# Asking earlier for the operands of a Strassen-Winograd down projection, on one Trainium2 core

## The chip, the core and the metric

The kernel runs on one core of a Trainium2 chip. The metric is the device time of one execution in microseconds (us); a median of several runs stands for it. The engines are TensorE (PE, its weight loads PEld), VectorE (DVE), ScalarE (ACT), GpSimd (POOL) and SyncE (SP), which here issues the DMAs.

## The reference

One layer of a hybrid decoder on 512 tokens of 2048 channels, in float32:

```python
x = x + mix @ w_out[l]          # mix: two attentions and a convolution module
h2 = _rms_norm(x, norm2_g[l])
x = x + (jax.nn.silu(h2 @ w_gate[l]) * (h2 @ w_up[l])) @ w_down[l]
```

w_gate and w_up are 2048 x 5632, w_down is 5632 x 2048. The change concerns the last line alone.

## The kernel before

**The products.** Gate, up and down are each done as one level of Strassen-Winograd: a 2 x 2 block product with seven multiplications, numbered 1 to 7, whose operands are sums of blocks. Each multiplication keeps float32 accuracy by splitting both operands into a high and a low part (`wh`, `wl` for the weights) and spending three matmuls of 128x128 by 128x512: high by high, low by high, high by low. POOL makes the sums of weight blocks (L172), ACT the high parts (L269 `wn` in PSUM, L270 `wh`), DVE the low parts (L271 `wl`), always two units ahead of PE. A unit is one pair (`wh`, `wl`), with 12 matmuls, or 6 where it holds one 128-row pair of blocks in place of two.

**Gate and up** (`class Up`) run as 11 blocks n of 28 units: seven products twice (`blk.first` 0 and 4), two units each. What a block gives is weighted on POOL (L1258), turned on DVE (L1262) and stored to DRAM as `bd` (L1267). Later each half of it becomes a `Pair` p (0 to 21): eight reads of `bd` in 32-row pieces with turned axes (`p..l`, `p..r`, L1131), sums on POOL (L1144 to L1149), the split into seven pieces on ACT (L1112) and POOL (L1116), and the stores of these pieces to `od` (L1101). A piece a*q*_*p*, 128x512, is the operand of Down's product q for pair p.

**Down** (`class Down`) runs as 12 blocks t of seven products in the order 7, 1, 5, 6, 4, 2, 3, two units each. Blocks 2r and 2r + 1 use the pairs of range r: four pairs (0 to 3), three (4 to 6), four, three, four, four. The first of the two uses its pieces for one half of the output and the second lets go of them after the other half. The results are added into 16 sums `y`, which start as the turned residual in DRAM (`x2t`, loaded at L1312). Because seven weight tensors of a block live in a few buffers, a block's weights are loaded to buffers as the splits of other weights leave them (L243).

**What sets the order around the change.** `load_next(n, limit)` (L1302 ff.) takes the next n entries of the list `feed` and issues a DMA for each on SP: pieces (L1317) or sums `y` (L1312). The list begins with range 0's 28 pieces, with eight `y` after the products 7 and 1, then the other eight `y`, then the pieces of range 1, 2 and so on. In the last block of gate and up (n = 10) it is called after each unit from the fifth on; in Down after each unit with n = 1, as long as fewer than 46 pieces are held. `later(k, f, queue=extras)` puts a call k units ahead; the last block's two `Pair`s, 20 and 21, are started that way (L1240 to L1242).

SP issues all these DMAs in the order of the program: weight loads, pieces, `y`, reads of `bd`, stores to `od`. An entry whose buffer is not free holds up all behind it. The program gives SP's DMAs eight semaphores in turn, and each DMA waits until the one eight before it has landed. Pieces, `y` and the tiles of a `Pair` share 73 slots of 128x512.

Of the kernel before, what the change touches and what calls it, by code (L numbers as in the profile page):

```python
# [71 lines left out]
NBLOCKS = NP // 2  # L72
# [44 lines left out]
def kernel(ctx: ExitStack, tc: tile.TileContext, xT, wi, wo, wgu, wd, cst_in, outT):  # L117
# [20 lines left out]
    def slot(name, dt=F32, cols=T):  # L138
        return sp.tile([P, cols], dt, name=name, tag="s")
# [66 lines left out]
    for t, (g, r) in enumerate(DOWN):  # L206
        first, end = RANGES[r]
# [227 lines left out]
    for k in range(KT):  # L435
# [5 lines left out]
        if k == 0:  # L441

            at["use"] = 2
            first = [splits.pop(u) for u in range(2)]
# [15 lines left out]
        if k == 0:  # L460
# [5 lines left out]
            first = w = None  # L466
# [613 lines left out]
    def norm2():  # L1080

        b = psum["high"].tile([P, 1024], F32, name="r2s", tag="h")[:, :NT]
        n2["r"] = token_scale(ssum2, D, "n2", b)[1]
# [19 lines left out]
    def later(n, fn, *args, queue=evacs):  # L1103
        while len(queue) <= n:
            queue.append([])
        queue[n].append((fn, *args))
# [59 lines left out]
    class Up:  # L1166
# [43 lines left out]
        def done(self, first, q, banks):  # L1210
            if first and q == 7:
                self.c = {}
            by = self.keep if first else self.add
            for a, b in enumerate(banks):
                if q == 7:
                    by(1, 1, a, b)
                elif q == 1:
                    by(0, 0, a, b)
                elif q == 4:
                    by(1, 0, a, b)  # L1220
                elif q == 6:
                    by(0, 1, a, b)
                    self.less(0, a, b)
                    self.less(1, a, b)
                elif q == 5:
                    self.less(1, a, b)
                else:
                    self.add(0, q - 2, a, b)
            if first:
                return  # L1230
            if q in (6, 5):
                later(1, self.gate, 6 - q, queue=extras)
            elif q == 2:
                self.dram = tc.dram_tile([T, T], F32, name=f"bd{self.n}")
            if q in (2, 3):
                later(0, self.weigh, q - 2)
                later(2, self.turn, q - 2)
                later(3, self.store, q - 2, queue=extras)
            if q == 3:
                first, every = (25, 20) if self.n == NBLOCKS - 1 else (5, 13)  # L1240
                for at in range(2):
                    later(first + every * at, Pair, self.dram, 2 * self.n + at, at, queue=extras)  # L1242

# [43 lines left out]
    def turn_x2(key):  # L1287

        z = turns[key] = slot("z")
        for part in range(4):  # L1290
            nc.sync.dma_start(by_blocks(z, part), turned(x2d, key, part))
# [14 lines left out]
    def load_next(n, limit=99):  # L1306
        while feed and n and len(acts) < limit:
            key = feed.pop(0)
            n -= 1
            if len(key) == 4:  # L1310
                y[key] = slot("y")
                nc.sync.dma_start(y[key], x2t[key])  # L1312
            else:
                q, j = key
                acts[key] = slot(f"a{q}_{j}", F32R)
                at = LAID.index(q)
                nc.sync.dma_start(acts[key].bitcast(F32), od[j][:, at * T:(at + 1) * T])  # L1317

    for n in range(NBLOCKS):
        blk = Up(n)  # L1320
        for blk.first in (0, 4):
            for i, q in enumerate(ORDER):
                for c, _ in enumerate(blk.product(q)):
                    at_unit = (7 if blk.first else 0) * 2 + 2 * i + c
                    if ticks.due and at_unit % 2:
                        ticks.tick()
                    if n == 0 and at_unit == 12:
                        norm2()
                    if 1 <= n <= 8 and at_unit in (9, 23):
                        key = SUMS[2 * n - 2 + at_unit // 16]  # L1330
                        turn_x2(key)
                        later(6, turn_x2_now, key)
                    if n == NBLOCKS - 1 and at_unit > 3:
                        load_next(1)
                if n == NBLOCKS - 1:
                    for j in range(4):
                        ops.pop((q, blk.first + j))
# [240 lines left out]
```

## Time and profile before

| | |
|---|---|
| time, median of 3 runs | 1874.56 us (1872.96 to 1874.84) |
| profiled execution, its own time | 1872.51 us |
| its span | 1870.6 us |
| mean granted TensorE clock | 0.997 |
| PE busy | 1846.8 us, 99% of the span |
| DVE, ACT, POOL busy | 77%, 71%, 59% |
| HBM traffic over the span | 171 GB/s |
| Down, first to last matmul | 1422.3 to 1866.3 us of the span |

A row of the timeline reads: start, duration, engine, line, operation, names, and in brackets the idle time of the engine just before it and what ended it. A row of the windows view gives for a stretch of the span the busy time of each engine, the granted TensorE clock, the mean busy share of the DMA engines and the bytes that they moved per second. Rows of SPq are issues of DMAs; their duration is that of the issue and not of the transfer. In the chain of waits a DMA's piece runs from issue to landing.

### The profile page before, as it was taken

How to read it: one execution, taken by the hardware profiler on the slowest of the kernel's cores; microseconds unless marked ns; L12 is line 12 of the kernel's file. 1: busy time of each engine (PE TensorE's matmuls, PEld its weight loads, DVE VectorE, ACT ScalarE, POOL GpSimd, SP SyncE). 2: the span in 40 equal slices, each digit the busy share in tenths (PEclk: the TensorE clock that was granted, in tenths of full speed). 3: DMA queues.
4: the chain of work that ended last, by engine and by line, in shares of the span. 5: the costliest groups of instructions: out<-in, count | busy, mean ns of one | idle time of the engine just before them, and what ended most of it. 6: DMA issues, size and time to landing. Idle time of an engine off the chain costs nothing.

```text
span 1870.6 us, 26605 instructions
## 1 busy us (share of the span) xinstructions
PE 1846.8 (99%) x8370; PEld 1528.0 (82%) x8370; DVE 1432.9 (77%) x2052; ACT 1322.3 (71%) x1794; POOL 1106.7 (59%) x850
## 2 busy tenths in 40 slices
PE   9999999999999999999999999999999989899999
PEld 7888888888888888888888888888888768688887
DVE  6678878998689777777777777777777656677777
ACT  6345644553468778888888888888888667778775
POOL 0126533100003567776887777868778778878775
PEclk9999999999999999999999999999999999999999
DMA  7252253343343366786777776777588676766655
GB/s 272 69 153 82 84 144 98 94 127 123 130 141 109 107 168 175 200 223 175 208 207 193 210 203 189 213 184 220 164 266 262 220 238 197 247 218 232 221 185 113
DMA packets 382988, 330.36 MB, mean 177 GB/s; under 512 B 171648, under 2 KB 311552, under 8 KB 382848
## 3 DMA queue, kind: packets, MB, share of 16 engines
q1 hardware_dynamic: 382704, 328.66, 60.2%
q8 instruction: 66, 1.08, 0.2%
q14 instruction: 74, 0.61, 0.1%
q10 hardware_dynamic: 144, 0.01, 0.0%
HBM read 255.56 MB, written 64.63 MB: 171 GB/s over the span
## 4 chain that ended last, share of the span: by engine, by line
PE 93%; DMA 4%; POOL 1%; ACT 1%; issue 0%; SPq 0%; DVE 0%; POOLq 0%; ACTq 0%; DVEq 0%
PE out L1184 15%; PE out L1182 15%; PE out L1185 15%; PE out L1432 6%; PE out L1433 6%; PE out L1434 6%; PE o L310 3%; PE o L309 3%; PE o L308 3%; DMA a<-od 2%; PE cq L308 1%; PE cq L309 1%; PE cq L310 1%; PE ak L308 1%; PE aq L308 1%; PE av L308 1%
## 5 line engine op out<-in xcount | busy, mean ns | idle before, releaser
L1182 PE MATMUL out<-wh,h 128*128 128x512 f32 x1232 | 479.4, 389 | 0.0
L1185 PE MATMUL out<-wh,h 128*128 128x512 f32 x1232 | 479.3, 389 | 0.0
L1184 PE MATMUL out<-wl,h 128*128 128x512 f32 x1232 | 479.3, 389 | 0.0
L1182 PEld LDWEIGHTS out<-wh,h 128*128 128x128 f32 x1232 | 231.2, 188 | 48.1
L1184 PEld LDWEIGHTS out<-wl,h 128*128 128x128 f32 x1232 | 231.2, 188 | 48.0
L1185 PEld LDWEIGHTS out<-wh,h 128*128 128x128 f32 x1232 | 231.2, 188 | 47.9
L1432 PE MATMUL out<-wh,a 128*128 128x512 f32 x620 | 243.5, 393 | 15.7 <-DMA a<-od 12.1
L1433 PE MATMUL out<-wl,a 128*128 128x512 f32 x620 | 242.1, 390 | 0.5 <-DVE wl L271 0.5
L1434 PE MATMUL out<-wh,a 128*128 128x512 f32 x620 | 241.8, 390 | 0.0
L275 ACT CAST wh<-w 128x1024 fp32r<-128x1024 f32 (+2 forms) x94 | 97.0, 1033 | 152.2 <-PE o L309 64.7
L1432 PEld LDWEIGHTS out<-wh,a 128*128 128x128 f32 x620 | 117.2, 189 | 44.8 <-DMA a<-od 10.7
L253 DVE TENSOR_TENSOR wl<-w,wh 128x1024 fp32r<-128x1024 f32 (+2 forms) x95 | 113.4, 1193 | 40.6 <-ACT wh L275 37.8
L1433 PEld LDWEIGHTS out<-wl,a 128*128 128x128 f32 x620 | 117.4, 189 | 25.0 <-DVE wl L271 1.3
L1434 PEld LDWEIGHTS out<-wh,a 128*128 128x128 f32 x620 | 117.3, 189 | 24.4
L1442 DVE TENSOR_TENSOR y<-y,out 128x512 f32<-128x512 f32 x164 | 106.4, 684 | 35.8 <-PE out L1434 31.2
L519 DVE SCALAR_TENSOR_TENSOR y<-bu,cst,y 128x511 f32<-128x511 f32 (+14 forms) x120 | 90.0, 750 | 0.7
L308 PE MATMUL o<-mh_c,wh 128*128 128x512 f32 x128 | 51.1, 399 | 0.0
L308 PE MATMUL cq<-hh,wh 128*128 128x512 f32 x128 | 50.5, 395 | 0.0
L310 PE MATMUL o<-mh_c,wl 128*128 128x512 f32 x128 | 50.0, 391 | 0.0
L309 PE MATMUL cq<-hl,wh 128*128 128x512 f32 x128 | 49.9, 390 | 0.0
L309 PE MATMUL o<-ml_c,wh 128*128 128x512 f32 x128 | 49.9, 390 | 0.0
L310 PE MATMUL cq<-hh,wl 128*128 128x512 f32 x128 | 49.9, 390 | 0.0
(2376 smaller groups left out, 4883.1 us busy)
## 6 DMA issues: line engine op xcount, KB each, us to landing
od<-a SPq DMA_DIRECT2D x154, 256.0 KB, 4.2
a<-od SPq DMA_DIRECT2D x154, 256.0 KB, 5.8
w<-in_wi SPq DMA_DIRECT2D x58, 512.0 KB, 3.5
w<-in_wo SPq DMA_DIRECT2D x32, 512.0 KB, 3.4
x<-in_xT SPq DMA_DIRECT2D x16, 256.0 KB, 6.9
xr<-in_xT SPq DMA_DIRECT2D x16, 256.0 KB, 3.7
x2d<-xr SPq DMA_DIRECT2D x16, 256.0 KB, 2.0
z<-x2d SPq DMA_DIRECT2D x64, 64.0 KB, 4.0
```

The lines of the kernel that those rows point to most:

```text
L253: fn(*args)
L275: (nc.vector.tensor_copy if u == 0 else nc.scalar.copy)(hi[:, :n], t[:, :n])
L308: nc.tensor.matmul(out, wh, xh, start=start, stop=False)
L309: nc.tensor.matmul(out, wh, xl, start=False, stop=False)
L310: nc.tensor.matmul(out, wl, xh, start=False, stop=stop)
L1182: nc.tensor.matmul(b, x[:, high], wh[:, s], start=c == f == 0 and q in (7, 1, 5, 2), stop=False, skip_group_check=True)
L1184: nc.tensor.matmul(b, x[:, high], wl[:, s], start=False, stop=False, skip_group_check=True)
L1185: nc.tensor.matmul(b, x[:, low], wh[:, s], start=False, stop=c == f == 1, skip_group_check=True)
L1432: nc.tensor.matmul(b[:, lo:hi], x[:, high], wh[:, s], start=start, stop=False, skip_group_check=True)
L1433: nc.tensor.matmul(b[:, lo:hi], x[:, high], wl[:, s], start=False, stop=False, skip_group_check=True)
L1434: nc.tensor.matmul(b[:, lo:hi], x[:, low], wh[:, s], start=False, stop=last, skip_group_check=True)
L1442: getattr(eng, op)(t, t, src)
```

## The change

Two numbers change. In the last block of gate and up, `load_next` takes one and two entries in turn, so that 36 entries are asked for there in place of 24: all of range 0's pieces and eight `y`. And the last block's two `Pair`s start 34 and 54 units after the block, in place of 25 and 45.

```diff
             if q == 3:
-                first, every = (25, 20) if self.n == NBLOCKS - 1 else (5, 13)
+                first, every = (34, 20) if self.n == NBLOCKS - 1 else (5, 13)
                 for at in range(2):
                     later(first + every * at, Pair, self.dram, 2 * self.n + at, at, queue=extras)
...
                     if n == NBLOCKS - 1 and at_unit > 3:
-                        load_next(1)
+                        load_next(1 + at_unit % 2)
```

As Down's own rule of one entry a unit stays, every entry of the list that follows stands 12 units further ahead. No instruction is added or taken away. The order on PE and DVE is the same; it changes on SP, and on ACT and POOL by the two `Pair`s.

SP at the end of gate and up's last block, before. In a name such as a4_2 the first number is the product, the second the pair; w('22', 'd0B') is a weight block of Down's block 0, b10c the last block's result.

```order
L243 DMA w('22', 'd0B')_13886<-in_wd 128x4x256
L1317 DMA a6_2_13906<-od2_5904 128x512
L1317 DMA a6_3_13928<-od3_5905 128x512
L1317 DMA a4_0_13951<-od0_5902 128x512
L1317 DMA a4_1_13980<-od1_5903 128x512
L1267 DMA bd10_13885<-b10c100_13340 128x512
L1267 DMA bd10_13885<-b10c101_13342 128x512
L243 DMA w('12', 'd0A')_13999<-in_wd 128x4x256
L1317 DMA a4_2_14013<-od2_5904 128x512
```

The same place of the changed kernel:

```order
L243 DMA w('22', 'd0B')_13908<-in_wd 128x4x256
L1317 DMA a3_1_13928<-od1_5903 128x512
L1317 DMA a3_2_13950<-od2_5904 128x512
L1317 DMA a3_3_13952<-od3_5905 128x512
L1312 DMA y_13975<-x2t1100_5932 128x512
L1312 DMA y_14004<-x2t1101_5933 128x512
L1267 DMA bd10_13907<-b10c100_13342 128x512
L1267 DMA bd10_13907<-b10c101_13344 128x512
L243 DMA w('12', 'd0A')_14023<-in_wd 128x4x256
```

Down's block 0 ends with a3_3. Before, ten pieces from a4_2 to a3_3 stand behind the store of `bd` and the load of w('12', 'd0A'); now all stand ahead of both.

SP around the weights of Down's block 4 (pairs 7 to 10), before; p21l and p21r are the reads of `Pair` 21.

```order
L243 DMA w('21', 'd4A')_15049<-in_wd 128x4x256
L1317 DMA a1_7_15057<-od7_5909 128x512
L1101 DMA od20_5922<-a4_20_14991 128x512
L1317 DMA a1_8_15082<-od8_5910 128x512
L1131 DMA p21l_15084<-bd10_13885 32x16x32 x4
L1317 DMA a1_9_15102<-od9_5911 128x512
L243 DMA w('11', 'd4A')_15115<-in_wd 128x4x256
L243 DMA w('21', 'd4B')_15117<-in_wd 128x4x256
L1317 DMA a1_10_15131<-od10_5912 128x512
L1131 DMA p21r_15133<-bd10_13885 32x16x32 x4
L243 DMA w('11', 'd4B')_15145<-in_wd 128x4x256
```

And in the changed kernel:

```order
L243 DMA w('21', 'd4A')_15045<-in_wd 128x4x256
L1317 DMA a4_7_15053<-od7_5909 128x512
L1317 DMA a4_8_15081<-od8_5910 128x512
L1317 DMA a4_9_15098<-od9_5911 128x512
L243 DMA w('11', 'd4A')_15115<-in_wd 128x4x256
L243 DMA w('21', 'd4B')_15117<-in_wd 128x4x256
L1317 DMA a4_10_15131<-od10_5912 128x512
L1101 DMA od20_5922<-a2_20_15055 128x512
L1101 DMA od20_5922<-a3_20_15057 128x512
L243 DMA w('11', 'd4B')_15145<-in_wd 128x4x256
```

The pieces next to these weights are now those of the fifth product and no longer of the second, and the eight reads of `Pair` 21 are gone from between the weights.

POOL at the end of Down's block 3, before (the rows from the last sum for block 3 to the first sums for block 4; d3u is a result of product 1):

```order
L172 TENSOR_TENSOR w('11', 'd3B')_14810<-w('11', 'd3B')_14810,w('12', 'd3B')_15047 128x512
L1442 TENSOR_TENSOR y_13481<-y_13481,d3u0_15060 128x512
L1442 TENSOR_TENSOR y_13507<-y_13507,d3u1_15062 128x512
L172 TENSOR_TENSOR w('s', 'd4A')_15194<-w('21', 'd4A')_15049,w('11', 'd4A')_15115 128x1024
L172 TENSOR_TENSOR w('s', 'd4B')_15220<-w('21', 'd4B')_15117,w('11', 'd4B')_15145 128x1024
```

And in the changed kernel:

```order
L172 TENSOR_TENSOR w('11', 'd3B')_14824<-w('11', 'd3B')_14824,w('12', 'd3B')_15043 128x512
L1116 TENSOR_TENSOR a5_20_15155<-p20a_15032,a5_20_15155 128x4x2x32
L1116 TENSOR_TENSOR a6_20_15157<-p20a_15032,a6_20_15157 128x4x2x32
L1442 TENSOR_TENSOR y_13433<-y_13433,d3u0_15059 128x512
L1442 TENSOR_TENSOR y_13461<-y_13461,d3u1_15061 128x512
L172 TENSOR_TENSOR w('s', 'd4A')_15204<-w('21', 'd4A')_15045,w('11', 'd4A')_15115 128x1024
L172 TENSOR_TENSOR w('s', 'd4B')_15232<-w('21', 'd4B')_15117,w('11', 'd4B')_15145 128x1024
```

Between the sum of w('11', 'd3A') with w('21', 'd3A') and the first sum for block 4, w('s', 'd4A'), one POOL instruction of `Pair` 20 stood before (its last, a4_20); now the other ten stand there, and a4_20 follows w('s', 'd4B'). Those of `Pair` 21 move from the first to the second half of block 4 and the start of block 5.

## The prediction

> **What bounds the kernel now.** The first page gives the shares.
>
> ```profile
> PE 1846.8 (99%) x8370; PEld 1528.0 (82%) x8370; DVE 1432.9 (77%) x2052; ACT 1322.3 (71%) x1794; POOL 1106.7 (59%) x850
> ```
>
> TensorE is busy for 1846.8 of 1870.6 us, so work on another engine counts only where TensorE waits for it. What TensorE waits for in Down is summed in the waits view (total, times, longest), from which these are all the rows of the lines 1432 to 1434.
>
> ```profile
> PE out L1432 <- DMA a<-od: 12.1, 8, 2.4
> PE out L1432 <- ACT wh L270: 1.9, 2, 1.5
> PE out L1432 <- ACT wn L269: 1.6, 1, 1.6
> ...
> PE out L1433 <- DVE wl L271: 0.5, 1, 0.5
> ```
>
> In all 16.1 us and twelve waits, all between Down's first matmul and its block 5. Some of them in TensorE's rows of the timeline, and the first matmul of block 5:
>
> ```profile
> 1455.21 0.50 PE L1432 MATMUL out<-wh,a 128*128 128x512 f32 x1 [2.17 <-DMA a<-od]
> ...
> 1525.43 0.47 PE L1432 MATMUL out<-wh,a 128*128 128x512 f32 x1 [1.64 <-ACT wn L269]
> ...
> 1533.51 0.77 PE L1432 MATMUL out<-wh,a 128*128 128x512 f32 x1 [2.21 <-DMA a<-od]
> ...
> 1604.27 0.50 PE L1432 MATMUL out<-wh,a 128*128 128x512 f32 x1 [2.38 <-DMA a<-od]
> ...
> 1617.61 0.39 PE L1432 MATMUL out<-wh,a 128*128 128x512 f32 x1
> ```
>
> Eight waits are for pieces, with 12.1 us. I count the one at 1525.43 as a ninth although the view names ACT's L269: the piece that this matmul reads was issued as late as 1519.90 (below). So pieces cost 13.7 us; the three others are for a split (1.9 + 0.5 = 2.4 us). The nine lie at the ends of blocks 0, 2 and 4, the first blocks of a range. The windows view tells the rest of the loss, since matmuls behind a wait are also slower.
>
> ```profile
> 1422.00:1465.00 43.00, 39.06 (x171) 31.60 (x171) 29.23 (x34) 30.87 (x37) 41.56 (x29) 1.00 0.81 285
> 1465.00:1503.00 38.00, 38.00 (x168) 31.16 (x167) 26.13 (x30) 27.76 (x30) 27.00 (x16) 1.00 0.58 178
> 1503.00:1542.00 39.00, 32.32 (x129) 24.96 (x129) 22.87 (x30) 23.84 (x36) 31.58 (x26) 0.91 0.73 238
> 1570.50:1617.50 47.00, 41.46 (x169) 32.13 (x168) 28.13 (x32) 33.08 (x40) 45.01 (x32) 0.96 0.76 263
> 1537.00:1540.00 3.00, 3.00 (x7) 2.41 (x8) 0.00 (x0) 0.00 (x0) 1.43 (x2) 0.50 1.05 399
> ```
>
> The second row is block 1, without a wait: 38.00 / 168 = 0.226 us for a matmul. In the first, third and fourth TensorE is idle for 3.94 + 6.68 + 5.54 = 16.16 us, which is the twelve waits. Their matmuls take 39.06 + 32.32 + 41.46 = 112.84 us; 171 + 129 + 169 = 469 of them at 0.226 would take 106.1. So 6.7 us more go in slower matmuls: about half of it at the first matmul behind each wait (0.50 us in place of 0.39 as at 1617.61, and one start's overlap, 0.39 - 0.23, lost: 0.27 each, 3.2 for twelve), the other 3.5 us in two stretches in which the granted clock was 0.50: one around the last row (0.91 in the third window), one late in the fourth (0.96). **Waits and what follows them cost 16.2 + 6.7 = 22.9 us**, and no more is to be had in blocks 0 to 4.
>
> **Why pieces are late.** The queue of SP, at the end of gate and up's last block and in block 0:
>
> ```profile
> 1418.00 3.42 SPq L1317 DMA_DIRECT2D a<-od  x4
> 1425.00 0.91 SPq L1267 DMA_DIRECT2D bd<-b10c  x2
> 1434.33 0.38 SPq L243 DMA_DIRECT2D w('12', 'd0A')_13999<-in_wd  x1
> ...
> 1446.96 1.13 SPq L1317 DMA_DIRECT2D a<-od  x2
> ```
>
> After four pieces SP stands from 1421.4 until the last block's result can be stored (1425.00), then until 1434.33, when the buffer of w('12', 'd0A') comes free. Ten pieces of block 0 are behind. They then go out in a burst, and the chain of waits shows what a DMA costs in it:
>
> ```profile
> 1440.77 6.13 DMA od<-a
> ...
> 1446.96 8.20 DMA a<-od
> ```
>
> SP can't issue a DMA before the one eight ahead of it has landed: the store issued at 1440.77 lands at 1446.90, and the piece issued at 1446.96 takes 8.20 us and ends TensorE's wait at 1455.21. Eight issues in 1446.96 - 1440.77 = 6.19 us make 0.77 us for each. In blocks 2 and 4 the queue is short, but one entry a unit comes out of the list while a product of two units uses four (or three) pieces; the lead is spent at the block's end:
>
> ```profile
> 1510.70 0.40 SPq L243 DMA_DIRECT2D w('12', 'd2A')_14700<-in_wd  x1
> 1519.90 0.50 SPq L1317 DMA_DIRECT2D a<-od  x1
> ```
>
> The piece for the matmul at 1525.43 is asked for 5.5 us ahead, and a piece takes this long from issue to landing:
>
> ```profile
> a<-od SPq DMA_DIRECT2D x154, 256.0 KB, 5.8
> ```
>
> **The change, first term: all pieces earlier.** The order shows block 0's last piece, a3_3, ahead of the store at 1425.00, with its use in the last unit ahead of 1465, block 1's first matmul: over 30 us. a3_6, block 2's last, now stands ahead of w('12', 'd2A') (1510.70), some 20 us before its use; a3_10 stands ahead of w('12', 'd4A'):
>
> ```profile
> 1583.60 0.38 SPq L243 DMA_DIRECT2D w('12', 'd4A')_15343<-in_wd  x1
> ```
>
> over 20 us before block 4's last product. Against 5.8 us, or 8.2 in a burst, all nine waits go, with their starts (9 x 0.27 = 2.4) and the clock stretches that lie between them (3.5): 13.7 + 2.4 + 3.5 = **19.6 us**. Buffers don't hold this up: each moved piece takes the slot of one that TensorE let go of at least 15 us before its new place in the queue.
>
> **Second term: the `Pair`s.** The splits at 1573.71 to 1595.70 are late because POOL is:
>
> ```profile
> 1553.67 3.45 SPq L1131 DMA_DIRECT2D p21l<-bd  x4
> 1560.74 3.34 SPq L1131 DMA_DIRECT2D p21r<-bd  x4
> 1564.20 1.31 SPq L243 DMA_DIRECT2D w('11', 'd4B')_15145<-in_wd  x1
> ...
> 1558.77 2.56 POOL L1442 TENSOR_TENSOR y<-y,d3u 128x512 f32<-128x512 f32 x2 [1.60 <-DVE d3u L1458]
> 1563.24 2.40 POOL L172 TENSOR_TENSOR w('s', 'd4A')_15194<-w('21', 'd4A')_15049,w('11', 'd4A')_15115 128x1024 f32<-128x1024 f32 x1 [1.92 <-DMA w('11', 'd4A')_15115<-in_wd]
> 1569.24 2.39 POOL L172 TENSOR_TENSOR w('s', 'd4B')_15220<-w('21', 'd4B')_15117,w('11', 'd4B')_15145 128x1024 f32<-128x1024 f32 x1 [3.60 <-DMA w('11', 'd4B')_15145<-in_wd]
> ...
> 1574.08 0.74 POOL L1144 TENSOR_TENSOR p21a<-p21l 128x256 f32<-128x256 f32 x1
> ...
> 1586.04 1.44 POOL L1116 TENSOR_TENSOR a<-p21r,a 128x256 fp32r<-128x256 f32 x2
> ```
>
> Eight turned reads of `Pair` 21 hold SP for 3.45 + 3.34 us between block 4's weights, w('11', 'd4B') goes out at 1564.20, and POOL is idle 3.60 us for it. After that POOL is behind through block 4. The reads now come later, and `Pair` 21's sums go behind those that are needed. So the three split waits go: 2.4 + 3 x 0.27 = **3.2 us**. Against that, ten POOL instructions of `Pair` 20 now stand in block 3 ahead of w('s', 'd4A'), and one less behind: three sums and L1149 at 0.74, six splits (L1116) at 0.72, together 7.3, less the 0.74 that a4_20 took there. POOL's idle times of 1.60 and 1.92 us absorb half: 6.5 - 3.5 = 3.0 us, so w('s', 'd4A') is done at 1563.24 + 2.40 + 3.0 = 1568.6. ACT needs 2.0 us more for `wn` and `wh`, and block 4's first matmul stood at 1570.5 (where the fourth window begins): a wait of 0.1 to 0.3, with 0.27 for the start. Its bounds are 0 and 6.5 + 1565.6 + 2.0 - 1570.5 + 0.27 = 3.9 if POOL can use neither idle time. I take **0.6 us** lost. w('s', 'd4B') follows at 1571.0, where it was done at 1571.63 before: nothing further.
>
> **Third term: twelve more transfers in gate and up's last block.**
>
> ```profile
> 1384.00:1422.00 38.00, 38.00 (x169) 31.49 (x168) 28.55 (x32) 31.85 (x39) 29.44 (x21) 1.00 0.91 280
> ```
>
> This stretch has the busiest DMA engines before Down, 0.91. In it, by the timeline of POOL, ACT and TensorE:
>
> ```profile
> 1385.85 2.41 POOL L172 TENSOR_TENSOR w('21', 'u21A')_13257<-w('21', 'u21A')_13257,w('22', 'u21A')_13486 128x1024 f32<-128x1024 f32 x1 [6.50 <-DMA w('22', 'u21A')_13486<-in_wgu]
> 1396.61 1.05 ACT L270 CAST wh<-w('11', 'u21A')_13374 128x1024 fp32r<-128x1024 f32 x1
> 1400.51 0.39 PE L1182 MATMUL out<-wh,h 128*128 128x512 f32 x1
> ```
>
> POOL has waited 6.50 us for w('22', 'u21A'), and in the chain behind it the first high part is done at 1397.66 and used at 1400.51: 2.85 us to spare. By the order, three or four more pieces now stand ahead of that weight; at 0.77 us it lands 2.3 to 3.1 us later, and TensorE waits 0 to 0.3 with 0.27 for the start. The price of a transfer has bounds: 0.26 MB / 280 GB/s = 0.94 from this row, and 8.20 / 8 = 1.03 from the burst. At 1.03 four make 4.1 and the loss is 1.5 us; at the other end it is nothing. I take **0.4 us**. The remaining transfers are absorbed while SP stands from 1421.4 on. Block 0's first weights are two transfers later (1.5 us), and have room:
>
> ```profile
> 1431.88 2.42 POOL L172 TENSOR_TENSOR w('11', 'd0A')_13743<-w('21', 'd0A')_13636,w('11', 'd0A')_13743 128x1024 f32<-128x1024 f32 x1
> 1435.28 1.05 ACT L270 CAST wh<-w('11', 'd0A')_13743 128x1024 fp32r<-128x1024 f32 x1
> 1438.59 0.39 PE L1432 MATMUL out<-wh,a 128*128 128x512 f32 x1
> ```
>
> The high part is done at 1436.33, 2.26 us before its use: nothing.
>
> *The Trainium skill, "DMA: Bandwidth & Descriptors", section Specifications, gives an HBM limit of about 358 GB/s for a core. With nine pieces more in the 38 us, the 280 GB/s of the row become 280 + 9 x 0.262 MB / 38 us = 342, and by that limit nothing would be late at all; by the row's share of 0.91 the same bytes would need 1.11 of the DMA engines, some 4 us more than there are. The clock stretch above moved 399 GB/s at a share of 1.05, so the trace does not agree with the limit, and I go by the price of a transfer.*
>
> **The sum.** 19.6 + 3.2 - 0.6 - 0.4 = 21.8 us. From the profiled execution's own 1872.51 us: 1850.7. The median of the runs shown, 1874.56, is 2.05 above that execution: 1852.8, rounded 1853.
>
> **Rivals.**
>
> *POOL becomes the bound in blocks 3 and 4.* Block 3 lasts 28.6 us; POOL then has four sums of 128x1024 at 2.40, four half as large at about 1.2, eight additions at 1.28 and `Pair` 20's 7.3: 31.9 us. For it: 31.9 is over 28.6, by 3.3; a second shortage of the same size could come with `Pair` 21 at block 5's start. Against it: it has 5 us of lead at the block's start and the two idle times. It would give back 3.3 to 6.6 us: 1856.1 to 1859.4, in the middle 1857.8.
>
> *The half clock stays.* The trace ties 0.50 to stretches with two waits close together, and block 0, with a wait of 2.17 us, had 1.00. If it has another cause, 3.5 us stay: 1856.3. *The Trainium skill, "TensorE: Matmul & The Clock Gate", Part 1, has the clock fall after an idle window of about 3.4 us. No wait here is that long, 2.4 being the longest, yet the clock fell: by that rule the waits would not be the cause. The trace speaks more for waits, since no row outside their neighbourhood has 0.50.*
>
> *Only block 0 heals.* Down's own limit, 46 pieces held, could eat the twelve entries of lead by block 2. Then only 3.94 + 0.5 go, less 0.4: 1870.5. Against it: the order has the places after block 0 moved too.
>
> *The change doesn't do what it says.* If the DMA engines are what makes pieces late in blocks 2 and 4 (1.05 in the stretch at 0.50), asking earlier only moves the queue: 1874, no change.
>
> *Slower: weights of up's last block queue behind the twelve transfers.* One mechanism: each added piece ahead delays w('22', 'u21A') and all behind it by its price, and TensorE waits from 2.85 us on. To cancel 21.8 + 0.4 + 2.85, twelve transfers would have to cost 2.1 us each; 0.77 to 1.03 was measured. At 2.3 it gives 1876 to 1878.
>
> **How the numbers follow.** Forecast, 1853: 0.58. POOL: 0.18. Half clock: 0.06. Only block 0: 0.05. No change: 0.06. Slower: 0.04; something else, split among them: 0.03. The range reaches down to where all costs are nothing (1872.51 - 22.9 + 2.05 = 1851.7) and 2.7 below, for the runs' own 1.9 and shorter waits in later blocks that I haven't counted; upward to the POOL case with both shortages in full (1859.4), up's block at its upper end (1.1 more) and the spread of 2, about 1863; block 4's bound of 3.9 lies inside. It holds the first three cases. Faster by over 0.2% (3.7 us, about what a measurement of this kernel can tell from no change): 0.58 + 0.18 + 0.06 + 0.05 and a little of the rest, 0.88; within it 0.07; slower 0.05.
>
> **What would show it.** Right: TensorE's rows in blocks 0, 2 and 4 without a bracket from a<-od, block 0 to block 5's start shortened from 195 us (1422.3 to 1617.6) to about 172, no stretch at 0.50. The second term: POOL's w('s', 'd4B') without an idle time for DMA, and a bracket of under 0.5 us at block 4's first matmul. The third: a bracket at the product that uses w('11', 'u21A'), and nothing above 1.5 us. Wrong would be brackets from ACT or POOL of 4 us and more in blocks 3 to 5, or pieces still late there with the DMA share above 1.

## The result and the profile after

| | before | changed |
|---|---|---|
| median of the runs | 1873.76 us (4 runs) | 1853.13 us (4 runs, 1851.65 to 1853.89) |
| ratio, with its 95% interval | | 0.9889 (0.9872 to 0.9906) |
| profiled execution, its own time | 1872.51 us | 1851.65 us |
| TensorE's clock below full, inside Down | 1533.3 to 1540.1, 1605.0 to 1608.4 | 1546.1 to 1549.6 |
| first matmul of Down | 1422.27 | 1420.75 |

The changed kernel is 20.6 us faster, where 21.6 was forecast from the median shown then (1874.56). All that the waits view of the changed kernel lists for TensorE (total, times, longest):

```profile
PE idle L332 <- DVE ones L342: 1.1, 1, 1.1
PE out L1432 <- DVE y L1442: 0.9, 1, 0.9
PE out L1433 <- DVE wl L271: 0.7, 1, 0.7
PE sides L1397 <- DVE y L1411: 0.7, 1, 0.7
PE out L1432 <- ACT wh L270: 0.7, 1, 0.7
```

No row is left that waits for a<-od: 12.1 us in eight waits before. L332 and L1397 lie at the kernel's start and end. The three other waits follow each other in block 3; in the timeline of TensorE, with the first matmuls of blocks 3, 4 and 5:

```profile
1525.47 0.39 PE L1432 MATMUL out<-wh,a 128*128 128x512 f32 x1
...
1541.24 0.50 PE L1432 MATMUL out<-wh,a 128*128 128x512 f32 x1 [0.65 <-ACT wh L270]
...
1543.76 0.49 PE L1432 MATMUL out<-wh,a 128*128 128x512 f32 x1 [0.87 <-DVE y L1442]
...
1544.94 0.50 PE L1433 MATMUL out<-wl,a 128*128 128x512 f32 x1 [0.69 <-DVE wl L271]
...
1558.73 0.39 PE L1432 MATMUL out<-wh,a 128*128 128x512 f32 x1
...
1596.81 0.39 PE L1432 MATMUL out<-wh,a 128*128 128x512 f32 x1
```

The bracket at 1543.76 names DVE's addition, but w('22', 'd3A') came to ACT late as well: its high part was done at 1543.70 (the row of L270 is quoted below). The windows view, for the stretch before Down and for blocks 0, 3 and 4:

```profile
1384.00:1422.00 38.00, 38.00 (x169) 31.45 (x168) 28.04 (x33) 31.62 (x39) 29.41 (x22) 1.00 1.03 322
1420.70:1458.80 38.10, 38.10 (x169) 31.55 (x169) 27.70 (x34) 29.24 (x37) 35.58 (x28) 1.00 0.85 300
1525.40:1558.70 33.30, 31.09 (x128) 24.71 (x127) 21.90 (x29) 23.19 (x36) 30.64 (x25) 0.95 0.80 269
1558.70:1596.80 38.10, 38.10 (x169) 31.53 (x168) 28.20 (x32) 32.36 (x39) 37.94 (x28) 1.00 0.91 282
```

Blocks 0 and 4 have TensorE busy throughout. Block 3 has the idle 2.21 us of the three waits and a mean clock of 0.95. The first matmul of each block gives its length (before, it stood at 1422.27, 1464.91, 1503.28, 1541.92, 1570.48 and 1617.61):

| us | block 0 | 1 | 2 | 3 | 4 | sum |
|---|---|---|---|---|---|---|
| before | 42.64 | 38.37 | 38.64 | 28.56 | 47.13 | 195.34 |
| changed | 38.08 | 38.08 | 28.56 | 33.26 | 38.08 | 176.06 |
| difference | -4.56 | -0.29 | -10.08 | +4.70 | -9.05 | -19.28 |

So 24.0 us are gone from blocks 0, 1, 2 and 4, and 4.7 are given back in block 3. From block 5 on nothing differs. The two profiled executions are 20.86 us apart; the 1.5 us beyond the table lie ahead of Down, and not at the change: within the first 700 us TensorE was idle for 3.10 us in one and 1.12 in the other.

Where block 3's 4.70 us come from is seen on SP and POOL, in the changed kernel:

```profile
1515.16 3.44 SPq L1131 DMA_DIRECT2D p20l<-bd  x4
1520.86 1.97 SPq L1131 DMA_DIRECT2D p20r<-bd  x4
1522.94 1.06 SPq L243 DMA_DIRECT2D w('22', 'd3A')_14893<-in_wd  x1
...
1527.90 2.41 POOL L172 TENSOR_TENSOR w('21', 'd3A')_14739<-w('21', 'd3A')_14739,w('22', 'd3A')_14893 128x1024 f32<-128x1024 f32 x1 [4.39 <-DMA w('22', 'd3A')_14893<-in_wd]
...
1536.41 0.74 POOL L1144 TENSOR_TENSOR p20a<-p20l 128x256 f32<-128x256 f32 x1
...
1538.73 1.29 POOL L172 TENSOR_TENSOR w('11', 'd3B')_14824<-w('21', 'd3B')_14801,w('11', 'd3B')_14824 128x512 f32<-128x512 f32 x1
...
1540.05 0.59 ACT L269 CAST wn<-w('11', 'd3B')_14824 128x512 fp32r<-128x512 f32 x1 [3.19 <-POOL w('11', 'd3B')_14824 L172]
...
1542.66 1.04 ACT L270 CAST wh<-w('22', 'd3A')_14893 128x1024 fp32r<-128x1024 f32 x1
```

The eight turned reads of `Pair` 20 take SP for 3.44 and 1.97 us at the end of block 2, and w('22', 'd3A') goes out behind them at 1522.94. POOL waits 4.39 us for it. From there it is late, and `Pair` 20's own sums go ahead of w('11', 'd3B') at 1538.73. ACT waits 3.19 us for that sum, TensorE for ACT.

### The profile page after: what moved, and what is told of

Same layout as the page of the kernel before. It is cut to its first block, busy times and chain, and to the rows that moved or that the text cites. A ratio compares the mean times of both kernels' runs of the same rounds, so it can differ in the third digit from the quotient of the medians.

```text
span 1850.0 us, 26616 instructions
## 1 busy us (share of the span) xinstructions
PE 1841.9 (100%) x8370; PEld 1528.4 (83%) x8370; DVE 1431.4 (77%) x2052; ACT 1320.1 (71%) x1794; POOL 1103.2 (60%) x850
## 4 chain that ended last, share of the span: by engine, by line
PE 99%; DMA 0%; POOL 0%; DVE 0%; issue 0%; SPq 0%; ACT 0%; DVEq 0%; POOLq 0%; ACTq 0%
PE out L1184 15%; PE out L1182 15%; PE out L1185 15%; PE out L1433 7%; PE out L1432 7%; PE out L1434 7%; PE o L310 3%; PE o L309 3%; PE o L308 3%; PE cq L308 2%; PE cq L309 2%; PE cq L310 2%; PE ak L308 1%; PE aq L308 1%; PE av L308 1%; PE aq L310 1%
```

## The experiments

Block lengths below are again from the first matmul of each block, in one profiled execution of each kernel; 38.08 and 28.56 are the lengths without a wait. Each ratio is to the kernel before on the same chip.

### One half of the change at a time

The first kernel takes the loads alone.

```diff
-                first, every = (34, 20) if self.n == NBLOCKS - 1 else (5, 13)
+                first, every = (25, 20) if self.n == NBLOCKS - 1 else (5, 13)
```

> Only the loads of the change: 36 entries in the last block, the two Pairs at 25 and 45 units as before. If the loads are what the change gains by, and slots hold nothing up: no wait for a piece in blocks 0, 2 and 4, block 3 at its 28.6 us of before, block 4 longer than 38.1 by the split waits of before (2.4 to 3.2 us): about 1851.5 us, so 1 to 2 below the changed kernel. Rival (the Pairs had to move because their early tiles take slots from the pieces): pieces are issued late again and waits for a<-od return, 1856 or more.

Measured: 1857.42 us beside 1871.11, ratio 0.9927 (0.9913 to 0.9942). Blocks 0 to 4: 40.09, 38.08, 28.56, 30.01, 44.73. No wait for a piece, so slots hold nothing up; but 1851.5 us was expected, and block 4 is 6.65 us too long, where 3.2 at most was expected, and block 3 1.45.

```profile
1543.30 3.31 SPq L1131 DMA_DIRECT2D p21l<-bd  x4
...
1548.52 0.40 SPq L243 DMA_DIRECT2D w('11', 'd4A')_15139<-in_wd  x1
...
1550.07 4.59 SPq L1131 DMA_DIRECT2D p21r<-bd  x4
1554.77 1.46 SPq L243 DMA_DIRECT2D w('11', 'd4B')_15169<-in_wd  x1
...
1552.62 2.41 POOL L172 TENSOR_TENSOR w('s', 'd4A')_15218<-w('21', 'd4A')_15073,w('11', 'd4A')_15139 128x1024 f32<-128x1024 f32 x1 [3.17 <-DMA w('11', 'd4A')_15139<-in_wd]
1559.95 2.35 POOL L172 TENSOR_TENSOR w('s', 'd4B')_15244<-w('21', 'd4B')_15141,w('11', 'd4B')_15169 128x1024 f32<-128x1024 f32 x1 [4.92 <-DMA w('11', 'd4B')_15169<-in_wd]
...
1564.38 0.80 PE L1432 MATMUL out<-wh,a 128*128 128x512 f32 x1 [3.68 <-ACT wh L270]
```

In the kernel before, the same matmul of block 4 stands at:

```profile
1573.71 0.50 PE L1432 MATMUL out<-wh,a 128*128 128x512 f32 x1 [0.34 <-ACT wh L270]
```

The reads of `Pair` 21 stand between block 4's weights as before and hold SP for 3.31 and 4.59 us. But TensorE now comes to block 4 without having waited in blocks 0 and 2: the sum w('s', 'd4B') is done 4.49 us behind block 4's first matmul (1562.30 and 1557.81), before it was 1.15 (1571.63 and 1570.48). So the same late weight costs 3.68 us in place of 0.34, and TensorE's clock halves behind it. The waits for pieces had hidden this. Block 3's 1.45 us come without any wait for a weight on POOL in it: POOL has no idle time from 1519.2 to 1549.4, with seven splits and a sum of `Pair` 20, at their earlier place, in between.

The second kernel takes the `Pair`s alone.

```diff
-                        load_next(1 + at_unit % 2)
+                        load_next(1)
```

> Only the move of the Pairs: 34 and 54 units, 24 entries as before. If the loads carry the gain: blocks 0, 2 and 4 keep their waits for pieces, the split waits of block 4 go (-3.2), block 3 becomes 4.7 longer: 1873.8 - 3.2 + 4.7 = 1875 us, and up to 1880 if the turned reads of Pair 20 also hold late pieces of block 2. Rival (the reads of the Pairs are what makes the pieces late in blocks 2 and 4): the waits in block 4 shrink by half or more, 1866 or less.

Measured: 1864.17 us, ratio 0.9965 (0.9953 to 0.9977); blocks 42.21, 38.86, 36.98, 28.71, 40.77. One us more than before was expected, 6.9 less came. By the number it is the rival that was right (1866 or less), by the trace only in part. The waits for pieces stay in blocks 0 and 2 (1.79 and 1.74 us in block 0), as the first theory has it. But block 4 loses 6.4 of its 9.05, of which the splits are 3.2 and the half clock 1.7; and two waits for pieces are left there with 1.94 us, where three were with 3.17: they shrink by 1.2 us, less than the half that the rival names. Block 3 doesn't grow: block 2 still ends 8.4 us late, and this covers what `Pair` 20 does. POOL waits 3.45 us for w('22', 'd3A') here too, but its sum with it starts at 1531.48, 7.4 us ahead of block 3's first matmul; in the changed kernel it starts 2.4 us behind it.

The halves are worth 13.7 and 6.9 us, and by their sum the whole, but this is a coincidence: in the profiles they take 13.9 and 7.8 us from blocks 0 to 4, the whole 19.3. Block 3 grows by 1.45 and 0.15 us with one half, and by 4.70 with both.

### What makes block 3 longer

Two kernels take one part of `Pair` 20 out of block 3's way. In the first its reads are 9 units earlier, as before the change, and its sums where the change put them; in the second the reads stay and the sums go 12 units later.

```diff
-                first, every = (34, 20) if self.n == NBLOCKS - 1 else (5, 13)
+                first, every = (25, 29) if self.n == NBLOCKS - 1 else (5, 13)
...
-                later(at, fn, queue=extras)
+                later(at + 9 * (p == 20 and at > 2), fn, queue=extras)
```

> The changed kernel with the eight turned reads of Pair 20 at 25 and 27 units as before, its sums and splits where the change put them. Block 3 of the changed kernel is 33.26 us, 4.70 over its 28.56. Theory A (two things add up on POOL: 4.39 us of waiting for w('22','d3A'), which stands behind the reads on SP, and Pair 20's 7.3 us of work; either alone fits the slack): block 3 back at 28.6, about 1848.4 us. Theory B (POOL's work alone): block 3 stays at 32 to 33, 1852 to 1853. Theory C (the reads alone): 1848.4 as in A.

Measured: 1848.81 us, ratio 0.9882 (0.9866 to 0.9899); blocks 38.19, 38.08, 28.56, 28.87, 38.27. POOL no longer waits for w('22', 'd3A'), and one short wait is left, at block 4's first matmul:

```profile
1524.86 2.43 POOL L172 TENSOR_TENSOR w('21', 'd3A')_14749<-w('21', 'd3A')_14749,w('22', 'd3A')_14893 128x1024 f32<-128x1024 f32 x1
...
1554.98 0.50 PE L1432 MATMUL out<-wh,a 128*128 128x512 f32 x1 [0.15 <-ACT wh L270]
```

```diff
-                later(at, fn, queue=extras)
+                later(at + 12 * (p == 20 and at > 2), fn, queue=extras)
```

> The changed kernel with the reads of Pair 20 where the change put them, its sums and splits 12 units later, in block 4. Theory A: POOL still waits 4.4 us for w('22','d3A') but has w('11','d3B') at 1537.7 in place of 1540.0; block 3 at 28.6, about 1848.4 us. Theory B: the same. Theory C (the reads alone): block 3 stays at 32 to 33, 1852 to 1853. If block 4 then has too much work on POOL (Pair 20's and Pair 21's together, 14.6 us beside 29.6 in 38.1), it becomes longer by up to 6 us instead.

Measured: 1851.49 us, ratio 0.9896 (0.9881 to 0.9910); blocks 39.73, 38.08, 28.56, 28.69, 38.08, and block 5 has 41.05.

```profile
1528.67 2.40 POOL L172 TENSOR_TENSOR w('21', 'd3A')_14739<-w('21', 'd3A')_14739,w('22', 'd3A')_14893 128x1024 f32<-128x1024 f32 x1 [4.10 <-DMA w('22', 'd3A')_14893<-in_wd]
...
1537.17 1.29 POOL L172 TENSOR_TENSOR w('11', 'd3B')_14824<-w('21', 'd3B')_14801,w('11', 'd3B')_14824 128x512 f32<-128x512 f32 x1
...
1614.67 0.50 PE L1432 MATMUL out<-wh,a 128*128 128x512 f32 x1 [1.77 <-ACT wh L270]
```

POOL waits 4.10 us for the weight as in the changed kernel, and block 3 is whole all the same. So theory A holds for the places that the change gives them: neither the reads nor POOL's work is enough alone; together they are 4.70 us. At other places the work can be enough: the two `Pair`s in a row make block 5 longer by 3 us, and POOL waits for no weight there: it has no idle time from 1587.2 to 1623.0.

The kernel with the early reads and the changed kernel, side by side:

> The changed kernel once more, beside the next three: 1853 us, block 3 at 33.3 us, block 0 between 38.1 and 40.1 from execution to execution (its tightest split had 0.6 us left).

> The kernel with the reads of Pair 20 early once more, to compare it with the changed kernel on the same chip. If it gains what block 3 lost: 4.2 us below (4.70 less the 0.5 that block 4's first matmul waits): 1848.8 us. If its single measurement was a chip's difference: within 2 us of the changed kernel.

Measured: 1852.81 us (1852.21 to 1854.04) for the changed kernel, with blocks of 39.25, 38.08, 28.56, 32.33 and 38.60; 1848.98 us (1847.91 to 1849.92) with the reads early, with 39.89, 38.08, 28.56, 28.69 and 38.98. Of the 3.8 us between them 3.64 are block 3's.

### Both `Pair`s later still

```diff
-                first, every = (34, 20) if self.n == NBLOCKS - 1 else (5, 13)
+                first, every = (46, 14) if self.n == NBLOCKS - 1 else (5, 13)
```

> The changed kernel with the two Pairs starting 46 and 60 units after the block in place of 34 and 54, so that Pair 20's sums fall in block 4 and Pair 21's in block 5, both of four pairs; the turned reads fall in the second half of block 3 and in block 4. If block 3's 4.70 us come from Pair 20's reads in front of its weights and its work on POOL: block 3 at 28.6 and no new wait in blocks 4 and 5 (POOL 29.6 + 7.3 in 38.1 us each): 1848 to 1849 us. Rival (turned reads between the weights of any block make its splits late, as Pair 21's did to block 4): reads of Pair 20 between the weights of block 4 in block 3's second half, block 4 longer by 3 to 6 us, 1852 to 1854.

Measured: 1856.03 us, ratio 0.9908 (0.9893 to 0.9923). The rival's mechanism is what came, a block later than it said: block 3 is whole, block 4 has 39.77 (1.69 too long, where 3 to 6 were named) and block 5 43.63 (5.55 too long).

```profile
1587.14 4.96 SPq L1131 DMA_DIRECT2D p21r<-bd  x4
...
1596.11 0.47 SPq L243 DMA_DIRECT2D w('22', 'd5A')_15549<-in_wd  x1
...
1594.21 2.39 POOL L172 TENSOR_TENSOR w('s', 'd5B')_15566<-w('21', 'd5B')_15441,w('11', 'd5B')_15468 128x1024 f32<-128x1024 f32 x1 [3.09 <-DMA w('11', 'd5B')_15468<-in_wd]
...
1602.79 2.42 POOL L172 TENSOR_TENSOR w('21', 'd5A')_15349<-w('21', 'd5A')_15349,w('22', 'd5A')_15549 128x1024 f32<-128x1024 f32 x1 [3.70 <-DMA w('22', 'd5A')_15549<-in_wd]
```

The reads hold SP for 4.96 us between block 5's weights and POOL waits twice, 3.09 and 3.70 us, with a `Pair`'s work still to do. A sum of POOL's time over a block (37 us of 38) said that both fit; the places of the waits in it said that they don't.

### How many are asked for, and where

Twelve more in the last block of gate and up:

```diff
-                        load_next(1 + at_unit % 2)
+                        load_next(2)
```

> The changed kernel with two entries a unit in the last block of gate and up, 48 in place of 36. The rival on the slower side put a price on it: each transfer ahead of w('22','u21A') and block 0's weights delays them by 0.77 to 1.03 us. With 36 the tightest split of block 0 has 0.6 us left, and in two of five profiles it waited (block 0 longer by 1.6 to 2.0). With 48, by that price, w('22','d0A') comes 6 to 10 us later: block 0 longer by 5 to 9 us, 1858 to 1862 us. If the queue takes them up in its idle time: 1853 as before.

Measured: 1861.08 us, ratio 0.9935 (0.9920 to 0.9950); block 0 44.77, block 3 32.85, the rest without loss.

```profile
1425.30 2.37 POOL L172 TENSOR_TENSOR w('s', 'd0B')_13898<-w('21', 'd0B')_13779,w('11', 'd0B')_13819 128x1024 f32<-128x1024 f32 x1 [6.37 <-DMA w('11', 'd0B')_13819<-in_wd]
...
1401.10 0.50 PE L1182 MATMUL out<-wh,h 128*128 128x512 f32 x1 [0.73 <-ACT wh L270]
...
1413.14 0.50 PE L1184 MATMUL out<-wl,h 128*128 128x512 f32 x1 [0.57 <-DVE wl L271]
...
1429.75 0.51 PE L1432 MATMUL out<-wh,a 128*128 128x512 f32 x1 [2.94 <-ACT wh L270]
```

This is the mechanism of the rival on the slower side, and it is real: POOL waits 6.37 us for w('11', 'd0B') and TensorE 2.94 us for its split, and twice within gate and up's last block (1401.10 and 1413.14). The twelve further transfers cost some 8 us (1861.08 against 1853.13); the change's own twelve cost 0 to 2 in block 0, since, as far as these profiles tell, the slack of the splits was there to be used up. In the profiles that have 36 entries in this place block 0 took 38.08, 39.25, 40.09, 38.19, 39.89, 39.73 and 38.46 us, 39.1 in the mean.

Six entries more than before, where the change has twelve:

```diff
-                        load_next(1 + at_unit % 2)
+                        load_next(1 + (at_unit % 4 == 1))
```

> The changed kernel with 30 entries asked for in the last block of gate and up in place of 36: half the added lead. By the lead, a3_6 and a3_10 come out of the list six units later than with 36, 12 to 16 us, and are asked for 4 to 10 us ahead of use, where a piece takes 5.8: waits of 0 to 3 us at the ends of blocks 2 and 4, none in block 0; block 3 somewhat below 33.3 as block 2 ends later: 1852 to 1857 us. If the lead is not the mechanism and the whole of 36 is needed: waits as before, 1865 or more.

Measured: 1852.90 us beside 1872.76, ratio 0.9897 (0.9883 to 0.9912); blocks 39.24, 38.08, 28.56, 33.20, 38.08. Six more entries remove all nine waits as well as twelve do, at the low end of what was expected. Whether fewer would, was not tried. Beside the changed kernel's second measurement (1852.81) nothing is gained or lost, and block 0 was no shorter than with 36.

No more in gate and up, two a unit in Down (from the kernel before, with its `Pair`s):

```diff
-                    load_next(1, FEED)
+                    load_next(2, FEED)
```

> The kernel before with two entries a unit in place of one in Down (24 in the last block, Pairs at 25 and 45, the limit of 46 as before). If the lead alone makes the waits of blocks 2 and 4, and standing behind the store and w('12','d0A') makes block 0's: block 0 stays at 42 to 43 us, no waits for pieces in blocks 2 and 4, blocks 3 and 4 as with the loads alone (30.0 and 44.7): 1860 to 1864 us. If it matters that the loads are out of Down's way altogether: waits for pieces in blocks 2 and 4 stay, 1868 or more.

Measured: 1861.06 us, ratio 0.9932 (0.9917 to 0.9946); blocks 38.08, 39.98, 28.56, 33.87, 44.89. Blocks 2 and 4 came as expected. Block 3 was to have 30.0 us and has 3.9 more: `Pair` 20's reads and the pieces, two at a time, fill SP from 1497.0 on, w('12', 'd2A') goes out behind them at 1508.42, POOL waits 4.37 us for it in block 2, and `Pair` 20's work still stands ahead of block 3's sums. Block 1 is 1.9 us too long, of which nothing had been said; why stays open. Block 0 did not come as expected either: it has no wait at all, although the queue of SP stands as it did:

```profile
1423.63 0.91 SPq L1267 DMA_DIRECT2D bd<-b10c  x2
1433.08 0.38 SPq L243 DMA_DIRECT2D w('12', 'd0A')_14003<-in_wd  x1
1433.56 0.93 SPq L1317 DMA_DIRECT2D a<-od  x2
...
1436.48 0.92 SPq L1317 DMA_DIRECT2D a<-od  x2
...
1438.64 1.82 SPq L1317 DMA_DIRECT2D a<-od  x2
...
1443.20 0.98 SPq L1317 DMA_DIRECT2D a<-od  x2
```

Two more pieces are ahead of the store, and the eight behind it have gone out by 1444.2, while the piece for the matmul at 1455.21 went out at 1446.96 before. So the standing alone does not make block 0's pieces late; with it, one a unit does, as in blocks 2 and 4.

Two attempts at a better kernel start from the one with the early reads. The first asks for two a unit early in gate and up's last block:

```diff
-                        load_next(1 + at_unit % 2)
+                        load_next(2 if at_unit < 16 else 1)
```

> The kernel with the reads of Pair 20 early (1848.8 us) and the 36 entries of the last block asked for two a unit up to its unit 15 and one a unit after, so that its second half has 12 as before. If block 0's splits are late by the transfers that stand ahead of its weights: their slack is back at 1.8 to 2.3 us as before, block 0 at 38.1 in every run, 1847.5 to 1848.8 us. If the first half has no room: waits in gate and up's last block itself, above 1850.

Measured: 1849.55 us, ratio 0.9873 (0.9857 to 0.9890); blocks 38.71, 38.08, 28.56, 28.69, 38.27. This is between the two cases. Block 0 is 0.63 us too long, and the last block of gate and up has no room in its first half, as the second case says: two splits are late in it.

```profile
1399.85 0.50 PE L1182 MATMUL out<-wh,h 128*128 128x512 f32 x1 [0.78 <-ACT wh L270]
...
1411.88 0.50 PE L1184 MATMUL out<-wl,h 128*128 128x512 f32 x1 [0.58 <-DVE wl L271]
```

The second asks for six entries more ahead of Down's start and for seven more in block 0:

```diff
-                        load_next(1 + at_unit % 2)
+                        load_next(1 + (at_unit % 4 == 1))
...
-                    load_next(1, FEED)
+                    load_next(1 + (self.t == c == 0), FEED)
```

> Reads of Pair 20 early, 30 entries in the last block and two in place of one at the first unit of each of block 0's seven products: the lead of 36 from block 1 on with half the transfers ahead of block 0's weights. If block 0's uneven time comes from these transfers: 38.1 in block 0, 28.6 in block 2 and 38.3 in block 4, 1847.5 to 1848.5 us, not above the kernel with reads early alone. If the seven more in block 0 hold block 1's weights: block 1 up to 40 us as with two in all of Down, 1850.

Measured: 1848.04 us (1847.46 to 1849.83) beside 1872.76, ratio 0.9873 (0.9855 to 0.9891): blocks 38.08, 38.08, 28.56, 28.69, 38.26. This is the lowest of all; 0.9 us below the early reads alone is within their spread, and 4.8 us below the changed kernel is not. Block 0 is whole here, and had 39.24 us with the same 30 entries above; what it loses from profile to profile is not settled by one profile of each kernel.

## Why the prediction was right, point by point

**The number.** 1853 was forecast and 1853.13 measured. Of the parts, the gross gain was forecast at 22.8 us and is 24.0; the costs at 1.0 and are 4.7 in the profiled execution; 1.5 us of its gain are from ahead of Down. So three errors of 1.2 to 3.7 us nearly cancel. And the median of the kernel before came out at 1873.76, 0.8 below the one that the forecast started from. The hit to 0.13 us is luck, and says less than the table of blocks. Of the signs that were named, blocks 0 to 4 came to 176.06 us in place of about 172, and one stretch at half clock was left; TensorE waited for no piece, and for no split at block 4's first matmul or at the product that uses w('11', 'u21A').

**First term, right in mechanism.** All nine waits for pieces are gone, and the loads alone are enough for it. Its size can't be told apart from the second term's: together they were to be 22.8 us and are 24.0. Its account of block 0 was incomplete: SP standing behind the store and w('12', 'd0A') is not enough to make the pieces late there (two a unit in Down, with the same standing, leave no wait).

**Second term, right in the gain.** Block 4 has 38.08 us, and POOL no longer idles for w('11', 'd4B'). It matters more than was forecast: with the waits for pieces gone, but the `Pair`s left where they were, blocks 3 and 4 are 8.1 us too long, not 3.2, as the loads alone show.

**The step that failed: "ten POOL instructions of Pair 20 now stand in block 3 ahead of w('s', 'd4A')", priced at 0.6 us at block 4's first matmul.** It was mis-sized: 4.70 us, and the place was inside block 3. The working counted POOL's instructions and took POOL's idle time of the old trace as free to absorb them. It followed the turned reads of `Pair` 21 away from block 4's weights and did not follow those of `Pair` 20 to their new place, ahead of w('22', 'd3A'). They turned the idle time into a wait. And it set the delay against the old times, block 4 at 1570.5, though the first term brings TensorE there over 10 us earlier: with the waits of block 2 left in, as the `Pair`s alone have it, block 3 lost 0.15 us. With the reads back in their place, the rest is what was forecast: one wait of 0.15 us and its start at block 4's first matmul, 0.5 us in blocks 3 and 4 together (1.0 in its second profile).

**Third term, small as forecast, but in another place.** 0.4 us was expected in gate and up's last block, which lost nothing: w('22', 'u21A') was to land 2.3 to 3.1 us later, and POOL's sum with it starts 36.17 us ahead of Down's first matmul (1384.58 and 1420.75), where it was 36.42 before. But block 0 lost 0 to 2.0 from profile to profile, where nothing was expected. The forecast compared 1.5 us of delay with 2.26 us of slack at the high part of w('11', 'd0A'). The tightest splits were others: the low parts of w('21', 'd0B') and w('22', 'd0A'), which the experiments show waiting. The stretch before Down moved 322 GB/s at a busy share of 1.03 and lost nothing. The Trainium skill, "DMA: Bandwidth & Descriptors", section Specifications, gives a limit of about 358 GB/s for a core. Here the trace does not bear it out that nothing is late below that figure: with 48 entries TensorE waits twice in this stretch, at 310 GB/s. The share of the DMA engines is no better sign, since it is lower there (0.97):

```profile
1384.00:1422.00 38.00, 36.70 (x161) 29.68 (x160) 26.21 (x30) 28.92 (x36) 24.42 (x18) 1.00 0.97 310
```

**The rivals.** POOL as a bound was the nearest to what happened: block 3's loss of 4.7 lies in the range that it gave, but by POOL's waiting together with its work. The half clock went with the waits, and came back in block 3, where there were three of them close together. That two must stand close together, as this rival reads the old trace, does not hold: the second stretch of the kernel before fell behind a single wait, the 2.38 us at 1604.27. The lead did not run out at block 2; the limit of 46 was no hindrance. The slower side's mechanism showed in gate and up's last block only with 48 entries and with 36 asked for early.

## What to carry to other kernels

When one wait is removed, measure again what it covered: here the same late weight cost 0.34 us before and 3.68 us after the loads were early. Follow every instruction of a step that is moved through each queue that it enters, and ask at the new place what stands behind it; adding up an engine's work over a stage misses the waits that a DMA queue puts into it. And a lead of half the size can do as well: try the smallest change that removes the wait, since each transfer more stands ahead of something, although here twelve cost no more than six.

## What the runs showed of the hardware

TensorE's granted clock halved for 3.41 or 6.83 us after waits; in the kernel before and in the changed one no wait in Down was longer than 2.38 us. Below are the 3.41 us ahead of four such stretches, two in the kernel before, one in the changed kernel and one with the loads alone (behind a wait of 3.68 us), and then three stretches after which it stayed at 1.00, one in the kernel before and two with the `Pair`s alone. The number behind the comma is the time in which TensorE was busy:

```profile
1529.88:1533.29 3.41, 1.42 (x7) 0.84 (x5) 3.13 (x4) 3.26 (x6) 3.41 (x4) 1.00 0.82 253
1601.56:1604.97 3.41, 1.03 (x5) 0.61 (x4) 1.50 (x2) 1.70 (x2) 3.41 (x3) 1.00 1.08 362
```

```profile
1542.74:1546.15 3.41, 1.85 (x7) 1.20 (x7) 3.41 (x6) 3.41 (x6) 3.41 (x3) 1.00 0.97 329
```

```profile
1559.51:1562.92 3.41, 1.18 (x6) 0.64 (x4) 0.00 (x0) 0.59 (x1) 2.97 (x2) 1.00 0.95 333
```

```profile
1451.39:1454.80 3.41, 1.64 (x8) 1.02 (x6) 1.32 (x2) 1.76 (x3) 3.13 (x3) 1.00 1.07 384
```

```profile
1451.60:1455.00 3.40, 1.61 (x7) 1.35 (x8) 1.03 (x2) 1.37 (x2) 2.42 (x2) 1.00 1.06 389
1458.40:1461.80 3.40, 1.66 (x8) 1.05 (x7) 1.15 (x1) 1.96 (x2) 3.19 (x2) 1.00 0.83 304
```

It fell after 1.42, 1.03, 1.85 and 1.18 us of work and stayed after 1.64, 1.61 and 1.66. So the engine need not be idle throughout; half a stretch of waits is enough, in one piece or in several, and about half is also where it may go either way. Where the boundary lies is left open by these rows, since busy time counts the slower starts behind a wait as work. The Trainium skill, "TensorE: Matmul & The Clock Gate", Part 1, gives a window of 3413 ns, with which the lengths agree. It has the clock fall after an idle window; here it fell after windows that were busy for 30 to 54%.
